# A two-block sequence model on one core: the state space branch's steps and its tiles of b and c traced in the first phase, its pairs of heads in two halves

## The chip, the cores and the metric

The kernel runs on one core of one Trainium2 chip. The metric is the device time of one execution in microseconds. Before the change the median of three runs is 3561.74 us (3559.2 to 3566.45).

## The reference

Two blocks of a hybrid sequence model follow each other on 512 tokens of width 1024. The first has three branches (state space, rwkv, hgrn), each gated and projected, then a feed-forward layer; the second has two layers of four other branches. The change touches the state space branch of the first block alone. What it computes, cut to the core:

```python
def ssd_branch(z, xbc, dt_raw, conv_w, conv_b, dt_bias, a_log, d_skip, norm_w):
    xbc = silu(centred_depthwise_conv(xbc, conv_w, conv_b))      # 5 taps, 12 tiles of 128 features
    xs, bm, cm = split(xbc, [1024, 1024 + 256])                  # x: 8 tiles, b and c: 2 tiles each
    dt = softplus(dt_raw.reshape(b, L, 2, 16) + dt_bias)         # the steps, two directions
    a = -exp(a_log)
    y_f = ssd_chunked(xs, dt[:, :, 0], a[0], bm, cm)
    y_b = flip_t(ssd_chunked(flip_t(xs), flip_t(dt[:, :, 1]), a[1], flip_t(bm), flip_t(cm)))
    y = (y_f + y_b + xs * d_skip[:, None]) * silu(z)
    return rmsnorm(y, norm_w)

def ssd_chunked(x, dt, a, bm, cm):                               # chunks of 128 tokens
    a_cum = cumsum(dt * a)
    lmat = exp(where(tril, a_cum[q] - a_cum[s], -inf))
    y_diag = (cm @ bm.T * lmat) @ (x * dt)
    chunk_states = bm.T @ (x * dt * exp(a_cum[-1] - a_cum))
    prev = scan(s -> exp(a_cum[-1]) * s + chunk_state)
    return y_diag + (cm @ prev) * exp(a_cum)
```

## The kernel before

Activations lie with features on the partitions and the 512 tokens along them, so a tile is 128 features by 512 tokens. Each matrix product splits weights and activations into a high and a low half-precision part and takes three matmuls per block of 128: a tile of projected features (`fm_g`, lines 1182 to 1193) is 24 matmuls of 128x512 over eight blocks, into one bank of PSUM. A weight unit of 512 KB holds the eight blocks; `_emit_unit` loads it on SP's queue (line 1069) and splits it into `whi` on ScalarE (line 1078) and `wlo` on VectorE (line 1079). In this phase there is one bank `acc` for foreground tiles, so the next tile starts when VectorE has read the last one. Matmuls of the background write to two banks `bg0` and `bg1`.

A scheduler lays out each engine's instructions: those traced first have priority, and later ones are put into gaps that it expects. Each engine then works through its queue in that order. Buffers of a pool go around: a new tile of a tag waits for the last reader of the buffer that it gets, and a pool that is opened over a closed one waits for its last use. Work buffers (`w`) are eight in all.

The method `first` runs the first block. The first phase is `rwkv` with `hgrn` and the gates beside it. Then its pools close and those of the branches' outputs and of the state space branch (`ssd`, line 613) open. `ssd` traces, in this order:

- The steps (lines 621 to 662): load of `wdt` on GpSimd's queue (line 1012), its split, 96 small matmuls (lines 629 to 631), the softplus in some 20 small instructions (lines 636 to 642), cumulated steps by matmuls with `tri` (line 647), totals (line 648), a transpose (line 658) and a round trip through memory: `crd` is stored (line 662) and later read back into rows (`crow`, line 690, three buffers).
- Tiles of b and c: `conv_silu` (line 602) projects a tile, scales it into a padded buffer `xp` (line 248), takes five taps (one on ScalarE, line 607, four on VectorE, line 609) and the silu (ScalarE line 610, VectorE line 611).
- The loop over eight pairs of heads: the x tile (`conv_silu`), the loads of `crow`, four transposes (line 694), four scaled copies `xd` (line 702), four masks `pm` (ScalarE lines 711 and 712, VectorE line 713), 16 products into a bank (line 720), read by line 723 into `y`; for each direction the states (lines 729 to 741), their products (line 748), scaled (lines 752 and 753) and added by GpSimd (line 754); then the z tile, read from its bank by line 757, its silu (759, 760), the product (761), the split (1239 and 1243), and the square and its sum on GpSimd (lines 764 to 768).
- The sum of squares by matmuls (line 771), its inverse root, and that as rows (lines 1320 to 1322).

Traced behind `ssd` as background is `up`: the projections of the three branches, first of rwkv's output (operands `yrh`, `yrl`), then hgrn's (`ygh`, `ygl`), 96 matmuls each, then the state space branch's own (`ysh`, `ysl`), 192 matmuls, each tile read by VectorE (lines 1354 and 1356) and added by GpSimd (line 1358). The operands of rwkv and hgrn come back from memory (`yd`, line 955), the gates too (`ug`, line 1347, two buffers). `out_ffn` follows; its first matmuls read `mh` and `ml`.

Of the kernel before, what the change touches and what calls it, by code (L numbers as in the profile page):

```python
# [78 lines left out]
def odd_even(w):  # L79
# [20 lines left out]
    + [16, 17, 18, 19] + [t + j for j in range(8) for t in (8, 0)]  # L100
# [135 lines left out]
class First:  # L236
# [365 lines left out]
    def conv_silu(self, it, n, out):  # L602

        nc, v = self.nc, self.nc.vector
        xp = self.conv_pad(self.fmx(it), 2)
# [1 line left out]
        nc.scalar.activation(out=c, in_=xp[:, 0:T], func=AF.Identity, scale=self.col("scw", n), bias=self.col("scb", n))
        for q in range(1, 5):
            v.scalar_tensor_tensor(out=c, in0=xp[:, q:q + T], scalar=self.col("scw", 12 * q + n), in1=c, op0=ALU.mult, op1=ALU.add)
        nc.scalar.activation(out=out, in_=c, func=AF.Tanh, scale=0.5)  # L610
        v.scalar_tensor_tensor(out=out, in0=out, scalar=1.0, in1=c, op0=ALU.add, op1=ALU.mult)

    def ssd(self, yh, yl):

        nc, v, mm = self.nc, self.nc.vector, self.nc.tensor.matmul
        mid, small = self.mid, self.small
        self.dsk = self.t(mid, [128, 8], "dsk")
        v.tensor_scalar(out=self.dsk, in0=self.col("sd", 0, 8), scalar1=4.0, scalar2=None, op0=ALU.mult)
        it = self.block_iter("w1", 38, 20)

        wd = self.load(mid, "wdt", [128, 8, 32], nc.gpsimd)
        wdh, wdl = self.t(mid, [128, 8, 32], "wdh", F16), self.t(mid, [128, 8, 32], "wdl", F16)
        self.split(wdh, wdl, wd, WS)
        pd = self.b("acc")
# [298 lines left out]
    def first(self, next_gain):  # L923
        parts = lambda p, n, k: (self.t(p, [128, k, T], n + "h", F16), self.t(p, [128, k, T], n + "l", F16))
        pool = self.tc.tile_pool
        if True:
            gd = self.t(self.dram, [24, 128, T], "gd", bufs=1)
            yd = self.t(self.dram, [2, 2, 128, 4, T], "yd", F16, 1)
            with self.banks(acc=1, S=2, T=1, O=1, H=1), pool(name="f_rwkv", bufs=1) as mid, pool(name="f_rwkvs", bufs=2) as small:
# [1257 lines left out]
```

## Time and profile before

| | |
|---|---|
| median of three runs | 3561.74 us (3559.2 to 3566.45) |
| the profiled execution | 3568.91 us, its span 3567.2 us, granted clock 0.974 |
| TensorE matmuls (PE) | 3344.1 us busy, 94% of the span |
| VectorE (DVE) | 2736.6 us, 77% |
| ScalarE (ACT) | 1602.6 us, 45% |
| GpSimd (POOL) | 771.2 us, 22% |
| moved by DMA | 368.16 MB, 103 GB/s |

The share of an engine is a mean over the whole span; a stretch of the branch is read from tables of that stretch. PEclk is the clock that TensorE was granted, as a part of full speed. A row of the trace gives start, length, engine, line, operation, tiles, and in brackets the engine's idle time before it with what ended it. The ends of matmuls overlap: from one start to the next is less than a matmul's own length.

### The profile page before, as it was taken

What the parts mean: (1) busy time and instruction counts of PE and PEld (TensorE: products, weight loads), DVE (VectorE), ACT (ScalarE), POOL (GpSimd) and SP (SyncE); (2) the same over time, 40 slices, a digit from 0 to 9 for tenths busy, and PEclk for the clock granted to TensorE, in tenths of its full rate; (3) what the DMA queues carried; (4) which work ended last, traced back from release to release, by engine and by line L of the source; (5) the groups of instructions that cost most, each with busy time, mean ns of one, the idle gap of its engine ahead of it and who ended that gap; (6) DMA issues with size and microseconds to landing.
All of it is one profiled execution on the core that took longest, in us unless ns stands there. A gap on an engine that the chain in (4) does not pass through costs nothing.

```text
span 3567.2 us, 60900 instructions
## 1 busy us (share of the span) xinstructions
PE 3344.1 (94%) x23806; PEld 2055.0 (58%) x23806; DVE 2736.6 (77%) x5600; ACT 1602.6 (45%) x3001; POOL 771.2 (22%) x782
## 2 busy tenths in 40 slices
PE   8999999798899998999989999999999989999998
PEld 4566666554445577656545545567656545545567
DVE  6778777578777888688877768788688867767788
ACT  4233333255444444364456534444364456534444
POOL 1222223223332212111121032221111220132211
PEclk9899999899999999999999999999999999999999
DMA  4222213133243334322323353335322323353333
GB/s 149 78 60 69 80 46 92 66 113 119 80 163 106 100 105 131 118 74 75 103 87 109 107 162 101 105 115 165 107 74 72 106 87 103 112 167 118 107 101 95
DMA packets 151156, 368.16 MB, mean 103 GB/s; under 512 B 44098, under 2 KB 47428, under 8 KB 150868
## 3 DMA queue, kind: packets, MB, share of 16 engines
q1 hardware_dynamic: 117492, 336.03, 30.4%
q0 software_dynamic: 7680, 23.00, 2.0%
q10 hardware_dynamic: 25696, 5.25, 0.8%
q8 instruction: 186, 3.05, 0.4%
q14 instruction: 102, 0.84, 0.1%
HBM read 322.72 MB, written 40.04 MB: 102 GB/s over the span
## 4 chain that ended last, share of the span: by engine, by line
PE 44%; DVE 31%; issue 8%; ACT 7%; POOL 5%; DMA 4%; ACTq 0%; SPq 0%; DVEq 0%; POOLq 0%
PE bg L1190 4%; PE bg L1191 4%; PE bg L1189 4%; PE acc L1189 3%; PE acc L1190 3%; PE acc L1191 3%; DVE wlo L1079 3%; POOL w L1464 2%; DVE bw L1118 2%; DVE w L1464 2%; PE acc L1224 1%; PE acc L1450 1%; PE acc L1449 1%; PE acc L1448 1%; PE acc L1226 1%
## 5 line engine op out<-in xcount | busy, mean ns | idle before, releaser
L1189 PE MATMUL acc<-xh,whi 128*128 128x512 f16 x1224 | 472.2, 386 | 34.5 <-DVE w L757 18.0
L1190 PE MATMUL acc<-xl,whi 128*128 128x512 f16 x1224 | 472.0, 386 | 0.0
L1191 PE MATMUL acc<-xh,wlo 128*128 128x512 f16 x1224 | 471.2, 385 | 0.0
L1078 ACT ACTIVATE whi<-wst 128x1024 f16<-128x1024 f32 x264 | 276.7, 1051 | 327.8 <-PE acc L1190 164.6
L1079 DVE SCALAR_TENSOR_TENSOR wlo<-wst,whi 128x1024 f16<-128x1024 f32 x264 | 329.6, 1249 | 32.3 <-ACT whi L1078 30.9
L1190 PEld LDWEIGHTS <-whi 128*128 128x128 f16 x1824 | 180.4, 99 | 240.2 <-issue 54.9
L1191 PEld LDWEIGHTS <-wlo 128*128 128x128 f16 x1824 | 180.3, 99 | 210.8 <-issue 15.3
L1189 PEld LDWEIGHTS <-whi 128*128 128x128 f16 x1824 | 181.3, 99 | 200.3 <-issue 11.3
L1189 PE MATMUL bg<-xh,bhi 128*128 128x512 f16 x596 | 230.1, 386 | 5.8 <-DVE hk L811 5.7
L1191 PE MATMUL bg<-xh,blo 128*128 128x512 f16 x596 | 229.8, 386 | 4.5 <-DVE reset L310 4.5
L1190 PE MATMUL bg<-xl,bhi 128*128 128x512 f16 x596 | 229.5, 385 | 0.0
L1464 POOL TENSOR_TENSOR w<-w,w 128x512 f32<-128x512 f32 x66 | 121.8, 1846 | 403.9 <-DVE w L1464 331.8
L1224 PE MATMUL acc<-whi,xh 128*128 128x128 f16 x1152 | 195.0, 219 | 4.1 <-DVE xp L1782 2.2
L1226 PE MATMUL acc<-whi,xl 128*128 128x128 f16 x1152 | 195.0, 219 | 0.0
L1225 PE MATMUL acc<-wlo,xh 128*128 128x128 f16 x1152 | 195.0, 219 | 0.0
L1078 ACT ACTIVATE bhi<-bst 128x1024 f16<-128x1024 f32 (+1 forms) x132 | 121.9, 933 | 100.5 <-PE bg L1190 86.0
L1079 DVE SCALAR_TENSOR_TENSOR blo<-bst,bhi 128x1024 f16<-128x1024 f32 (+1 forms) x132 | 155.5, 1182 | 6.8 <-ACT bhi L1078 5.8
L1189 PE MATMUL bg<-xh,whi 128*128 128x512 f16 x408 | 158.1, 387 | 0.5 <-ACT bw L1334 0.5
L1190 PE MATMUL bg<-xl,whi 128*128 128x512 f16 x408 | 157.9, 387 | 0.0
L1191 PE MATMUL bg<-xh,wlo 128*128 128x512 f16 x408 | 157.7, 386 | 0.0
L1190 PEld LDWEIGHTS <-bhi 128*128 128x128 f16 x980 | 97.2, 99 | 105.0 <-issue 15.5
L1191 PEld LDWEIGHTS <-blo 128*128 128x128 f16 x980 | 96.8, 99 | 103.1 <-issue 7.1
(685 smaller groups left out, 9227.5 us busy)
## 6 DMA issues: line engine op xcount, KB each, us to landing
wst<-win SPq DMA_DIRECT2D x92, 512.0 KB, 3.5
bst<-win SPq DMA_DIRECT2D x64, 512.0 KB, 3.7
wst<-wff SPq DMA_DIRECT2D x60, 512.0 KB, 3.5
wst<-w SPq DMA_DIRECT2D x58, 512.0 KB, 3.6
gd<-bw SPq DMA_DIRECT2D x88, 256.0 KB, 2.1
ug<-gd SPq DMA_DIRECT2D x88, 256.0 KB, 2.8
wst<-wf SPq DMA_DIRECT2D x30, 512.0 KB, 3.4
bst<-w SPq DMA_DIRECT2D x20, 512.0 KB, 4.1
```

Source lines behind the costliest of these rows:

```text
L1078: nc.scalar.activation(out=hi[:, h], in_=st[:, h], func=AF.Copy, scale=WS)
L1079: nc.vector.scalar_tensor_tensor(out=lo[:, h], in0=st[:, h], scalar=WS, in1=hi[:, h], op0=ALU.mult, op1=ALU.subtract)
L1118: nc.vector.tensor_tensor(out=src, in0=x, in1=y, op=ALU.add if m == 1 else ALU.subtract)
L1189: mm(ps, lhsT=wh, rhs=h[:, k, :], start=(k == 0), stop=False)
L1190: mm(ps, lhsT=wh, rhs=l[:, k, :], start=False, stop=False)
L1191: mm(ps, lhsT=wl, rhs=h[:, k, :], start=False, stop=(k == nk - 1))
L1224: mm(o, lhsT=xh, rhs=wh, start=(k == 0), stop=False)
L1225: mm(o, lhsT=xh, rhs=wl, start=False, stop=False)
L1226: mm(o, lhsT=xl, rhs=wh, start=False, stop=(k == 7))
L1448: mm(ps, lhsT=ah[:, p], rhs=bh, start=start and p == 0, stop=False)
L1449: mm(ps, lhsT=ah[:, p], rhs=bl, start=False, stop=False)
L1464: tt = lambda eng, o, x, y, op=ALU.add: eng.tensor_tensor(out=o, in0=x, in1=y, op=op)
```

## The change

`conv_silu` is taken apart: `scaled` reads the tile from its bank into a work buffer, `conv` takes the five taps with shortened ranges at the ends and no pad, `silu2` does the silu. `ssd_begin` is called while the first phase's pools are open: it traces the steps, with work buffers and a bank of the first phase, loads `wdt` and `tri` on SP, and traces the tiles of b and c up to their taps. `ssd` takes these over, loads its own `tri`, and traces each pair's entry (x tile, rows, transposes, scaled copies) ahead of the pair before it; `xd` has eight buffers. The units of `w1` are reordered for this. The read-out of z gets high priority, and the squares move from GpSimd to ScalarE.

```diff
-    + [16, 17, 18, 19] + [t + j for j in range(8) for t in (8, 0)]
+    + [16, 17, 18, 19, 8] + [t + j for j in range(7) for t in (9, 0)] + [7]
...
-    def conv_silu(self, it, n, out):
-        xp = self.conv_pad(self.fmx(it), 2)
...
+    def scaled(self, it):
+        x = self.w()
+        self.nc.vector.tensor_tensor(out=x, in0=self.fmx(it), in1=self.rb, op=ALU.mult)
+        return x
+    def conv(self, x, n):
+        nc, v = self.nc, self.nc.vector
         c = self.w()
...
+        nc.scalar.activation(out=c, in_=x, func=AF.Identity, scale=self.col("scw", 24 + n), bias=self.col("scb", n))
+        for q in (0, 1, 3, 4):
+            to, by = slice(max(2 - q, 0), T - max(q - 2, 0)), slice(max(q - 2, 0), T - max(2 - q, 0))
+            v.scalar_tensor_tensor(out=c[:, to], in0=x[:, by], scalar=self.col("scw", 12 * q + n), in1=c[:, to], op0=ALU.mult, op1=ALU.add)
+        return c
...
-    def ssd(self, yh, yl):
+    def ssd_begin(self):
...
-        wd = self.load(mid, "wdt", [128, 8, 32], nc.gpsimd)
+        wd = self.w(256).rearrange("p (k c) -> p k c", k=8)
+        nc.sync.dma_start(out=wd, in_=self.io["wdt"])
...
-        pd = self.b("acc")
+        pd = self.b("S")
...
-        tri = self.load(mid, "tri", [128, 2, 128])
+        tri = self.w(256).rearrange("p (d c) -> p d c", d=2)
+        nc.sync.dma_start(out=tri, in_=self.io["tri"])
...
+        return it, (dt, cum, dec, tot, crd), [self.conv(self.scaled(it), 8 + n) for n in range(4)]
+    def ssd(self, yh, yl, begun):
+        it, (dt, cum, dec, tot, crd), bcx = begun
...
+        tri = self.load(mid, "tri", [128, 2, 128])
...
-            self.conv_silu(it, 8 + n, bc[:, n])
+            self.silu2(bcx[n], bc[:, n])
...
-        for j in range(8):
+        def enter(j):
             g = j // 4
             x = self.t(mid, [128, T], "xs", bufs=2)
-            self.conv_silu(it, j, x)
+            self.silu2(self.conv(self.scaled(it), j), x)
...
-                    t = self.t(mid, [128, T], "xd", bufs=4)
+                    t = self.t(mid, [128, T], "xd", bufs=8)
...
+            return x, crow, xd, xe
+        nxt = enter(0)
+        for j in range(8):
+            g = j // 4
+            x, crow, xd, xe = nxt
+            if j < 7:
+                nxt = enter(j + 1)
...
-            v.tensor_tensor(out=z, in0=pz, in1=self.rb, op=ALU.mult)
+            with self.tc.high_priority():
+                v.tensor_tensor(out=z, in0=pz, in1=self.rb, op=ALU.mult)
...
-                nc.gpsimd.tensor_tensor(out=sq, in0=y, in1=y, op=ALU.mult)
+                nc.scalar.activation(out=sq, in_=y, func=AF.Square)
...
                 beside(1000, 1000)
+                begun = self.ssd_begin()
...
-                    rbs = self.ssd(*ysm)
+                    rbs = self.ssd(*ysm, begun)
```

Where instructions stand is shown at three places. Lines of the kernel after lie some 30 further down: its 1101 is 1069 before, 987 is 955, 1221 is 1189, and in the loop 724 is 702, 753 is 723, 771 is 741, 783 is 753, 788 is 757.

TensorE's queue at the end of the first phase, before. `H` is the hgrn's bank, `T` that of the rwkv's last transposes, `xh` the operand of the steps' matmuls:

```order
L887 MATMUL H_6707<-hi_5719,hw_6705 128x128 x3
L584 MATMUL T_6603<-ident_75,M_5957 128x128 x4
L904 MATMUL H_6715<-hi_5719,hs_6170 128x128
L908 MATMUL H_6715<-hst_6711,hp_5578 128x128
```

The same place in the kernel after; `acc_6919` is the bank of b's first tile:

```order
L918 MATMUL H_6707<-hi_5719,hw_6705 128x128 x3
L1221 LDWEIGHTS whi_6534
L1221 MATMUL acc_6919<-xh,whi_6534 128x512
L1222 LDWEIGHTS whi_6534
L1222 MATMUL acc_6919<-xl,whi_6534 128x512
L584 MATMUL T_6603<-ident_75,M_5957 128x128
L1223 LDWEIGHTS wlo_6535
L1223 MATMUL acc_6919<-xh,wlo_6535 128x512
```

All 24 matmuls of b's first tile stand now between the rwkv's last chunk and the hgrn's last products (line 904 before, 935 after); the other three tiles of b and c stand behind the steps, and behind 32 matmuls of `up` that precede line 647.

SP's queue at the same time, before; `yd` holds the outputs of rwkv and hgrn in memory:

```order
L598 DMA yd_184<-w_6612 128x512
L599 DMA yd_184<-w_6613 128x512
L1012 DMA tri_6914<-tri 128x256
L955 DMA yrh_6760<-yd_184 128x2048
L598 DMA yd_184<-gyh_6740 128x512
L599 DMA yd_184<-gyl_6741 128x512
L955 DMA yrl_6761<-yd_184 128x2048
```

After:

```order
L598 DMA yd_184<-w_6612 128x512
L599 DMA yd_184<-w_6613 128x512
L631 DMA w_6751<-wdt 128x256
L1044 DMA tri_7098<-tri 128x256
L987 DMA yrh_7083<-yd_184 128x2048
L598 DMA yd_184<-gyh_6740 128x512
L599 DMA yd_184<-gyl_6741 128x512
L987 DMA yrl_7084<-yd_184 128x2048
```

The load of `wdt` has come to SP's queue, ahead of the first load into the new pools; the loads of `yrh` and `yrl` stand where they stood.

VectorE's queue in the loop, around the fourth pair's scaled copies, before (`xd`, `sst` and `sec` are all of the same pair):

```order
L611 SCALAR_TENSOR_TENSOR xs_7727<-xs_7727,w_7763 128x512
L702 TENSOR_TENSOR xd_7780<-T_7775,dt_6878 128x512
L702 TENSOR_TENSOR xd_7782<-T_7775,dec_6881 128x512
L702 TENSOR_TENSOR xd_7784<-T_7775,dt_6878 128x512
L702 TENSOR_TENSOR xd_7786<-T_7775,dec_6881 128x512
L736 COPY sst_7839<-S_7835 128x128
L741 SCALAR_TENSOR_TENSOR sst_7839<-sst_7839,tot_6927,S_7835 128x64 x4
L753 TENSOR_TENSOR sec_7852<-sec_7852,O_7845 128x384
```

After, around the fifth pair's copies; `sy_7878` and `sec_7897` are the fourth pair's, `w_7955` is its z tile:

```order
L621 SCALAR_TENSOR_TENSOR xs_7774<-xs_7774,w_7808 128x512
L753 SCALAR_TENSOR_TENSOR sy_7878<-xs_7582,dsk_7096,O_7861 128x512
L724 TENSOR_TENSOR xd_7825<-T_7820,dt_6854 128x512
L724 TENSOR_TENSOR xd_7827<-T_7820,dec_6856 128x512
L724 TENSOR_TENSOR xd_7829<-T_7820,dt_6854 128x512
L788 TENSOR_TENSOR w_7955<-acc_7924,rb_166 128x512
L724 TENSOR_TENSOR xd_7831<-T_7820,dec_6856 128x512
L783 TENSOR_TENSOR sec_7897<-sec_7897,O_7890 128x384
```

The copies of the next pair stand among the work of this one, and the read-out of z stands among the copies. Between the read-out of the first x tile and the sum of squares TensorE's queue held 220 matmuls of `up`; now it holds 106, with 58 before it (18 then) and 220 behind (146 then).

## Rows read from the trace of the kernel before

**Rows 1.** Busy time of each engine in four stretches; its first row names the columns
```profile
core 0: us, PE busy (x) PEld busy (x) DVE busy (x) ACT busy (x) POOL busy (x), PEclk, DMA share, GB/s
676.00:704.70 28.70, 13.54 (x138) 10.67 (x139) 10.04 (x42) 4.10 (x14) 7.62 (x11) 0.52 0.39 127
704.70:740.60 35.90, 35.00 (x178) 17.72 (x177) 30.83 (x59) 17.38 (x34) 3.19 (x13) 1.00 0.42 143
740.60:975.60 235.00, 206.06 (x1162) 114.74 (x1160) 182.37 (x289) 116.61 (x240) 73.05 (x67) 0.94 0.31 99
975.60:1013.30 37.70, 36.20 (x162) 17.31 (x163) 24.00 (x31) 10.88 (x15) 17.07 (x11) 0.91 0.37 119
```

**Rows 2.** TensorE in order of time at the hand-over; start, length, in brackets idle before
```profile
682.24 1.72 PE L584 MATMUL T<-ident,M 128*128 128x128 f32 x4 [3.08 <-DVE M L578]
...
693.84 1.09 PE L1571 MATMUL H<-ident,hw 128*128 128x128 f32 x4 [4.08 <-DVE hw L918]
...
700.63 0.21 PE L629 MATMUL acc<-wdh,xh 128*128 128x32 f16 x1 [5.71 <-ACT wdh L1239]
```

**Rows 3.** SP's queue in order of time, then DMA issues with KB and time to landing
```profile
688.92 0.32 SPq L599 DMA_DIRECT2D yd<-w  x1
...
696.92 0.42 SPq L955 DMA_DIRECT2D yrl<-yd  x1
...
yrl<-yd SPq DMA_DIRECT2D x1, 512.0 KB, 5.1
...
wdt<-wdt POOLq DMA_DIRECT2D x1, 128.0 KB, 4.9
```

**Rows 4.** TensorE in order of time: one tile's first and last matmul, what follows
```profile
704.74 0.38 PE L1189 MATMUL acc<-xh,whi 128*128 128x512 f16 x1
...
709.70 0.38 PE L1191 MATMUL acc<-xh,wlo 128*128 128x512 f16 x1
...
711.55 0.38 PE L1189 MATMUL acc<-xh,whi 128*128 128x512 f16 x1 [0.61 <-DVE xp L248]
...
713.35 1.96 PE L647 MATMUL O<-da,tri 128*128 128x16 f32 x16
```

**Rows 5.** First x tile read out, first matmul for the sum of squares, first of `out_ffn`
```profile
740.58 0.69 DVE L248 TENSOR_TENSOR xp<-acc,rb 128x512 f32<-128x512 f32 x1
...
975.57 1.05 PE L771 MATMUL T<-ones,sqa 128*128 128x1 f32 x8 [1.66 <-POOL sqa L768]
...
1013.35 0.38 PE L1189 MATMUL acc<-mh,whi 128*128 128x512 f16 x1
```

**Rows 6.** TensorE's groups from 740.6 to 975.6: busy us, mean ns, idle before, releaser
```profile
L1189 PE MATMUL acc<-xh,whi 128*128 128x512 f16 x120 | 48.8, 407 | 18.2 <-DVE w L757 18.0
...
L694 PE MATMUL T<-ident,xs 128*128 128x128 f32 x32 | 6.0, 320 | 7.3 <-DVE xs L611 7.2
```

**Rows 7.** VectorE's groups from 700 to 977, and line 761's first and last start
```profile
L753 DVE TENSOR_TENSOR sec<-sec,O 128x384 f32<-128x384 f32 x16 | 8.9, 554 | 11.4 <-PE O L748 7.9 <-ACT sec L752 3.5
...
L1079 DVE SCALAR_TENSOR_TENSOR blo<-bst,bhi 128x512 f16<-128x512 f32 x8 | 6.3, 782 | 0.0
L723 DVE SCALAR_TENSOR_TENSOR sy<-xs,dsk,O 128x512 f32<-128x512 f32 x8 | 6.0, 748 | 15.1 <-PE O L720 15.1
L761 DVE SCALAR_TENSOR_TENSOR sy<-sy,w 128x512 f32<-128x512 f32 x8 | 5.5, 687 | 4.9 <-POOL sy L754 4.9
...
L1356 DVE SCALAR_TENSOR_TENSOR mg<-ug,bg 128x512 f32<-128x512 f32 x8 | 5.4, 678 | 0.0
...
L761 DVE SCALAR_TENSOR_TENSOR sy<-sy,w x8: 677/692/693, 772.3 to 972.0; 128x512 f32<-128x512 f32 x8
```

**Rows 8.** GpSimd's squares as a group; one of them and a VectorE operation beside it
```profile
L767 POOL TENSOR_TENSOR w<-sy 128x512 f32<-128x512 f32 x7 | 10.6, 1514 | 6.5 <-DVE sy L761 6.5
...
797.76 1.95 POOL L767 TENSOR_TENSOR w<-sy 128x512 f32<-128x512 f32 x1 [1.24 <-DVE sy L761]
...
798.74 1.52 DVE L713 TENSOR_TENSOR pm<-pm,cb 128x512 f32<-128x512 f32 x1
```

More of the change, by code (lines that the diff above doesn't have):

```diff
@@ L599, in store @@
         self.nc.sync.dma_start(out=yd[1, :, j], in_=l)
-    def conv_silu(self, it, n, out):
+    def scaled(self, it):
[3 more added lines that the diff above has]
+    def conv(self, x, n):
         nc, v = self.nc, self.nc.vector
-        xp = self.conv_pad(self.fmx(it), 2)
         c = self.w()
[L607 to L611, printed above, removed]
@@ L613, in ssd, with silu2 @@
-    def ssd(self, yh, yl):
+        nc.scalar.activation(out=c, in_=x, func=AF.Identity, scale=self.col("scw", 24 + n), bias=self.col("scb", n))
[3 more added lines that the diff above has]
+        return c
+    def silu2(self, c, out):
+        self.nc.scalar.activation(out=out, in_=c, func=AF.Tanh, scale=0.5)
+        self.nc.vector.scalar_tensor_tensor(out=out, in0=out, scalar=1.0, in1=c, op0=ALU.add, op1=ALU.mult)
@@ L615, in ssd @@
+    def ssd_begin(self):
         nc, v, mm = self.nc, self.nc.vector, self.nc.tensor.matmul
-        mid, small = self.mid, self.small
-        self.dsk = self.t(mid, [128, 8], "dsk")
-        v.tensor_scalar(out=self.dsk, in0=self.col("sd", 0, 8), scalar1=4.0, scalar2=None, op0=ALU.mult)
         it = self.block_iter("w1", 38, 20)
-        wd = self.load(mid, "wdt", [128, 8, 32], nc.gpsimd)
-        wdh, wdl = self.t(mid, [128, 8, 32], "wdh", F16), self.t(mid, [128, 8, 32], "wdl", F16)
-        self.split(wdh, wdl, wd, WS)
@@ L624, in ssd @@
-        pd = self.b("acc")
+        flat = lambda a: a.rearrange("p k c -> p (k c)")
+        wd = self.w(256).rearrange("p (k c) -> p k c", k=8)
+        nc.sync.dma_start(out=wd, in_=self.io["wdt"])
+        wdh, wdl = (self.w(256, dt=F16).rearrange("p (k c) -> p k c", k=8) for _ in range(2))
+        self.split(flat(wdh), flat(wdl), flat(wd), WS)
+        pd = self.b("S")
         for i in range(4):
@@ L631, in ssd @@
                 mm(o, lhsT=xl, rhs=wdh[:, k], start=False, stop=(k == 7))
-        sm = lambda tag: self.t(small, [128, 4, 32], tag, bufs=1)
-        dt, da, cum, dec = sm("dt"), sm("da"), sm("cum"), sm("dec")
+        sm = lambda tag: self.t(self.norms, [128, 4, 32], tag)
+        dt, cum, dec, tot = sm("dt"), sm("cum"), sm("dec"), sm("tot")
+        da = self.w(128).rearrange("p (i c) -> p i c", i=4)
         fl = lambda a: a.rearrange("p i c -> p (i c)")
@@ L649, in ssd @@
         v.tensor_copy(out=fl(cum), in_=pc[:, 0:128])
-        tot = self.t(small, [128, 4, 32], "tot", bufs=1)
         v.tensor_copy(out=fl(tot), in_=pc[:, 128:256])
@@ L655, in ssd @@
         nc.scalar.activation(out=fl(tot), in_=fl(tot), func=AF.Exp)
-        pr = self.b("T")
+        pr = self.b("S")
         for i in range(4):
@@ L662, in ssd @@
         nc.gpsimd.dma_start(out=crd, in_=cr[0:32])
+        return it, (dt, cum, dec, tot, crd), [self.conv(self.scaled(it), 8 + n) for n in range(4)]
+    def ssd(self, yh, yl, begun):
+        nc, v, mm = self.nc, self.nc.vector, self.nc.tensor.matmul
+        mid, small = self.mid, self.small
+        it, (dt, cum, dec, tot, crd), bcx = begun
+        self.dsk = self.t(mid, [128, 8], "dsk")
+        v.tensor_scalar(out=self.dsk, in0=self.col("sd", 0, 8), scalar1=4.0, scalar2=None, op0=ALU.mult)
+        tri = self.load(mid, "tri", [128, 2, 128])
         bc = self.pwide(mid, "bc", 4)
@@ L763, in ssd @@
             if j == 0:
-                nc.gpsimd.tensor_tensor(out=sqa, in0=y, in1=y, op=ALU.mult)
+                nc.scalar.activation(out=sqa, in_=y, func=AF.Square)
             else:
                 sq = self.w()
-                nc.gpsimd.tensor_tensor(out=sq, in0=y, in1=y, op=ALU.mult)
+                nc.scalar.activation(out=sq, in_=y, func=AF.Square)
                 nc.gpsimd.tensor_tensor(out=sqa, in0=sqa, in1=sq, op=ALU.add)
@@ L1684, in values, with log_sigmoid @@
         return v
-    def log_sigmoid(self, out, f, n):
+    def log_sigmoid(self, out, f, n, t=None):
         nc, v = self.nc, self.nc.vector
-        t = lambda tag: self.t(self.small, [128, n], tag, bufs=1)
+        t = t or (lambda tag: self.t(self.small, [128, n], tag, bufs=1))
         a, s, w, p = t("lsa"), t("lss"), t("lsw"), t("lsp")
```

4 lines of the change are left out of this document (2 added, 2 removed).

## The prediction, made before the kernel after had run

> **What bounds the kernel now.** I first read the busy table by stretch [rows 1], cut at four events of the branch: the hand-over from the first phase (676 to 704.7 us), the steps and the tiles of b and c (to 740.6, where the branch's first x tile is read out of its bank), the loop over eight pairs (to 975.6, the matmuls of the sum of squares), and the tail of `up` (to 1013.3, where `out_ffn` begins). The built instructions stand in the same order on every engine before and after this region in both kernels, so the prediction is a sum over these stretches. TensorE is the engine that all wait for. It is busy 13.5 of 28.7 us in the hand-over, 35.0 of 35.9 in the second stretch, 206.1 of 235.0 in the loop, 36.2 of 37.7 in the tail. What can be won is its idle time, 28.9 us of the loop and about 15 of the hand-over, and what it does at the lower clock there (granted 0.52 in the hand-over, 0.94 in the loop). Second I read who ends the idle time. In the hand-over TensorE waits for the end of the rwkv and hgrn chains and last for `wdt`, 5.71 us [rows 2], because that load is issued behind the release of the first phase's pools and takes 4.9 us [rows 3]. In the loop the idle time before the tile matmuls is 18.2 us, 18.0 of it until line 757 has read the z tile out of the single acc bank; 7.3 us more come before the transposes of x [rows 6]. Third, VectorE: 182.4 us of 235 in the loop [rows 1], and it waits too, 15.1 us for the heads' matmuls, 11.4 for the states' (line 753), 4.9 for GpSimd (line 761) [rows 7]. One pair follows another every (972.0 - 772.3) / 7 = 28.5 us [rows 7], and no engine fills it: a pair's chain is too serial.
>
> **The hand-over.** A tile is 24 matmuls, and from the first to the last of a tile 23 starts take 4.96 us [rows 4], so 0.216 us each and 5.2 us a tile. The order now puts b's first tile between the transposes of line 584 and the hgrn matmuls, where TensorE idles 3.08 and 4.08 us at 0.5 clock and more [rows 2]. I cost it at nothing there; in twice the time, if the clock stays low, it would still fit, with at most some 1 us of delay for the chain. `wdt` is now loaded by SP right behind the yd store of 688.92 [rows 3] and lands, by the old 4.9 us, before 694. The 96 matmuls of the steps then wait only for the hgrn transpose (693.84) and the split on ScalarE behind it; by the transpose's 1.09 [rows 2] and, as an estimate, 1.3 for the two reads and the split behind it, they start at 696.2 and not 700.63: 4.4 us earlier. That is not all won: the next on TensorE's queue are matmuls of `up`, and their operand yrl is still issued at 696.92 and lands 5.1 us later [rows 3], at 702.0; its pool still waits for the first phase. So TensorE idles once more, some 2.7 us. Then 32 of these matmuls (6.9 us) precede line 647: 708.9, not 713.35 [rows 4], again 4.4 us earlier, bounded by TensorE's queue and not by VectorE. What is late next is the read-out of b's first tile. Its w buffer is the one that da held, so it comes behind the steps, about 713.9, and b's second tile starts at 714.0 where before it started at 711.55 [rows 4]. From that start to the read-out of the first x tile took 740.58 - 711.55 = 29.0 us [rows 4, 5], of which some 3 were line 647's and 658's own matmuls, now done: 26.0. **x's first tile is read out at 740.0, 0.6 us earlier.** But 58 matmuls of `up` are done by then, and 18 before.
>
> **The loop.** On TensorE the order leaves 106 matmuls of `up` in it, where 220 stood: 114 fewer, -24.6 us. Work: 206.1 - 24.6 = 181.5 us. The waits: the z read-out has high priority now, and TensorE has the next pair's x tile around it. Bounds: all 28.9 us stay, or none does. I replace the 18.0 by the least that such a read-out cost, 0.61 us [rows 4], eight times (4.9), and keep the other 10.9: 15.8. Loop by TensorE: 197.3 us. On VectorE: six read-outs of `up` fewer at 0.68 (line 1356) and six halves of weights fewer at 0.78 (line 1079) [rows 7] are -4.1 and -4.7. The squares leave GpSimd for ScalarE, which has room (116.6 us of 235 [rows 1]). When a square ran on GpSimd from 797.76 for 1.95 us, line 713 took 1.52 us from 798.74 [rows 8]; an operation of this size takes 0.69 (line 761 [rows 7]). The 0.83 for each of eight squares are -6.6; bounds 0 and the squares' whole time, 8 x 1.514 = 12.1 us [rows 8]. 182.4 - 4.1 - 4.7 - 6.6 = 167.0. Of its 52.6 us of waiting I keep those on a producer that still stands right ahead, 15.1 and 4.9, and 4.7 that no row names, and drop those for states, transposes and x tiles, since they now belong to the next pair and stand several rows ahead: 191.7. TensorE's 197.3 is the longer and holds; a pair then takes 24 us, not 28.5. Eight xd buffers let the next pair's copies be made before this pair's have been read. The conv's pad is gone with its memsets; its taps are the same five instructions. The second load of tri, and a weight remainder of `up` that now stands before crd on GpSimd's queue, I cost at nothing: tri is wanted at 708.9, crd at 713. **Loop: -37.7 us**; the sum of squares comes at 937.3, not 975.57 [rows 5].
>
> **The tail.** What left the loop has to be done here: 220 matmuls of `up` follow (220 x 0.216 = 47.5 us), 146 before. Before, it took 1013.35 - 975.57 = 37.8 us [rows 5], 31.5 of it for 146 matmuls; of the other 6.3, 1.5 were waits (36.2 busy of 37.7) and (1 - 0.91) x 37.7 = 3.4 the lower clock [rows 1]. Both go, since matmuls over yg now cover the chain from the sum of squares to its rows; 1.4 stays. 47.5 + 1.4 = 48.9: **+11.1 us.** `out_ffn` starts at 986.2.
>
> **Sum:** -0.6 - 37.7 + 11.1 = -27.2 us. The profiled execution took 3568.9 (span 3567.2, 1.7 outside it); it would take 3541.7. The median of the three runs is 7.2 lower, 3561.7, which gives 3534.5: **3535 us**.
>
> **A rule beside it.** The Trainium skill, "SBUF — State Buffer" (section "SBUF: two separate sides"), says that VectorE, in an operation with two SBUF inputs, and GpSimd share a port pair that one of them holds for its whole instruction, while the other waits. The trace agrees in kind: 1.52 us against 0.69 [rows 7, 8]. By the rule, as an estimate, a square could cost VectorE its full length, and the sum would be that of the second rival.
>
> **The rivals.** *The loop keeps its waits.* If TensorE's 28.9 us of idle time only change place, since there is still one acc bank and one for transposes, the loop is 181.5 + 28.9 = 210.4 us: -0.6 - 24.6 + 11.1 = -14.1, 3548 us. For it: each engine works in its queue's order, and two pairs in it only help where the order guessed durations right. *The squares held VectorE for their whole length.* Then 12.1 us go, VectorE's sum falls to 186.2, and with it those waits of TensorE that VectorE ends: 181.5 + 4.9 = 186.4 us, -0.6 - 48.6 + 11.1 = -38.1 in all, 3524 us. Against it: line 713 lost 0.83 of 1.95. *Slower: the filler is spent early.* `up` filled the loop, and 40 of its matmuls are now gone before x. If a pair's time is set by its own chain (heads, GpSimd's additions, then z) at 28.5 us whatever the order, the loop stays at 235 and the tail has grown: -0.6 + 11.1 = +10.5, 3572 us. It decides from a loop of 224.5 us, 27.2 a pair. For it: GpSimd's additions and the fourth pm still wait in turn, and crow has three buffers as before. Against it: VectorE's own 167 us leave a pair at 21. That the change doesn't do what it says is no rival of its own: the order shows it done.
>
> **How the numbers follow.** My forecast (3528 to 3543) has 0.50, the loop that keeps its waits (3543 to 3556) 0.22, the whole squares 0.15, and what lies above, no change or slower, 0.13. Two in ten left out: 3521 to 3557. About 0.2%, 7.1 us, is what a measurement of this kernel tells from no change: a loop under 217 us is faster (0.85), one of 217 to 231 is the same (0.08), a longer one slower (0.07).
>
> **What would show it.** In the profile after: `wdt` landing before 694 and the steps' matmuls at 696; a wait of some 2.7 us for yrl in front of `up`; line 647's matmuls near 709; the wait for the z read-out down from 18 us to about 5; a pair every 24 us; the sum of squares near 937 and `out_ffn` near 986; line 713 close to 0.7 us on average. I am wrong if the pairs still take 27 us or more, if TensorE waits in the loop for weights or for crow, or if the tail waits for weights of wbs rather than running through.

## The result and the profile after

| | before | after |
|---|---|---|
| median of seven runs each, us | 3566.45 (3559.2 to 3577.13) | 3532.95 (3517.86 to 3544.5) |
| ratio, with its 95% interval | | 0.9898, 0.988 to 0.9917 |
| profiled execution, us | 3568.91 | 3532.95 |
| its span, us | 3567.2 | 3531.2 |
| predicted, us | | 3535 (3521 to 3557) |

The kernel after is 1.0% faster, and its time is within 2 us of the forecast. The forecast change was smaller, -26.7 us from the 3561.74 known then; by the seven runs of each it is -33.5. That it came so near is partly luck: three terms of the sum were wrong by 4 to 14 us and largely cancelled.

Busy time of each engine in the kernel after, cut at the events of [rows 1]: the hand-over, the steps and the tiles of b and c up to the first x tile's read-out, the loop, the tail up to `out_ffn`.

```profile
core 0: us, PE busy (x) PEld busy (x) DVE busy (x) ACT busy (x) POOL busy (x), PEclk, DMA share, GB/s
676.00:704.70 28.70, 17.94 (x160) 11.28 (x158) 15.11 (x55) 5.31 (x16) 7.63 (x6) 0.71 0.49 156
704.70:744.30 39.60, 36.68 (x185) 18.36 (x183) 31.88 (x51) 19.49 (x37) 4.91 (x6) 0.99 0.48 158
744.30:927.80 183.50, 175.47 (x1050) 100.61 (x1048) 156.12 (x276) 112.43 (x238) 47.23 (x42) 0.99 0.30 98
927.80:981.80 54.00, 51.17 (x237) 24.23 (x237) 32.96 (x39) 15.19 (x20) 25.06 (x16) 0.97 0.45 146
```

The events themselves in order of time, answering to [rows 5], and below them the durations and the first and last start of line 792 (761 before), answering to the last of [rows 7]:

```profile
744.32 0.69 DVE L605 TENSOR_TENSOR w<-acc,rb 128x512 f32<-128x512 f32 x1
...
927.80 1.05 PE L802 MATMUL T<-ones,sqa 128*128 128x1 f32 x8
...
981.83 0.38 PE L1221 MATMUL acc<-mh,whi 128*128 128x512 f16 x1
```

```profile
L792 DVE SCALAR_TENSOR_TENSOR sy<-sy,w x8: 679/692/694, 775.4 to 924.4; 128x512 f32<-128x512 f32 x8
```

The first x tile is read out 3.7 us later than before, the loop takes 183.5 us and not 235.0, the tail 54.0 and not 37.8: -31.5 us up to `out_ffn`. A pair takes (924.4 - 775.4) / 7 = 21.3 us, 28.5 before. The other 4.5 us by which the spans differ lie behind `out_ffn`, in code that did not change; that part took 2553.8 us before, 2549.4 here and 2555.9 in a second profile of the kernel after, so it is no effect of the change.

In the loop, TensorE's and VectorE's groups that answer to [rows 6] and [rows 7] (busy us, mean ns, idle before, releaser):

```profile
L1221 PE MATMUL acc<-xh,whi 128*128 128x512 f16 x120 | 45.6, 380 | 1.1 <-DVE w L605 1.1
...
L750 PE MATMUL O<-pm,xd 128*64 128x128 f32 x256 | 31.2, 278 | 1.5 <-DVE pm L743 0.7 <-ACT ysh L1271 0.4 <-ACT w L798 0.3
L778 PE MATMUL O<-bc,sst 128*64 128x128 f32 x192 | 23.7, 283 | 1.8 <-DVE sst L771 1.8
...
L1223 PE MATMUL bg<-ygh,blo 128*128 128x512 f16 x22 | 8.9, 415 | 2.8 <-DVE blo L1111 2.8
...
L743 DVE TENSOR_TENSOR pm<-pm,cb 128x512 f32<-128x512 f32 x30 | 21.0, 713 | 1.1 <-ACT pm L742 1.1
...
L615 DVE SCALAR_TENSOR_TENSOR w<-w,cols,w 128x510 f32<-128x510 f32 x16 | 13.9, 866 | 0.9 <-ACT w L612 0.8
L615 DVE SCALAR_TENSOR_TENSOR w<-w,cols,w 128x511 f32<-128x511 f32 x16 | 11.9, 742 | 0.0
...
L1275 DVE SCALAR_TENSOR_TENSOR ysl<-sy,cols,ysh 128x512 f16<-128x512 f32 x8 | 7.8, 978 | 0.0
...
L753 DVE SCALAR_TENSOR_TENSOR sy<-xs,dsk,O 128x512 f32<-128x512 f32 x8 | 6.0, 748 | 15.9 <-PE O L750 15.9
```

The 18.2 us in front of the tile matmuls are 1.1 and no longer end with z. The same 120 matmuls are shown with a mean of 380 ns, 407 before, and the granted clock of the loop is 0.99, not 0.94. One pause of TensorE in the loop of the kernel before, and what follows it:

```profile
916.77 0.38 PE L1189 MATMUL bg<-ygh,bhi 128*128 128x512 f16 x1
919.55 0.59 PE L1189 MATMUL acc<-xh,whi 128*128 128x512 f16 x1 [2.40 <-DVE w L757]
919.93 0.63 PE L1190 MATMUL acc<-xl,whi 128*128 128x512 f16 x1
920.36 0.63 PE L1191 MATMUL acc<-xh,wlo 128*128 128x512 f16 x1
...
922.78 0.38 PE L1191 MATMUL acc<-xh,wlo 128*128 128x512 f16 x1
922.99 0.38 PE L1189 MATMUL acc<-xh,whi 128*128 128x512 f16 x1
```

Behind the pause the matmuls start 0.43 us apart, at the lower of the clock's two levels (1.2 GHz), and at the end 0.21 us apart again (2.4 GHz). With 8.0 us of pauses in the loop and not 28.9, less of it runs at the lower level. VectorE still waits 15.9 us for the heads' matmuls (line 753, 723 before).

### The profile page after: what moved, and what is told of

Same layout as the page of the kernel before. It is cut to its first block, busy times and chain, and to the rows that moved or that the text cites. A ratio compares the mean times of both kernels' runs of the same rounds, so it can differ in the third digit from the quotient of the medians.

```text
span 3531.2 us, 60877 instructions
## 1 busy us (share of the span) xinstructions
PE 3334.8 (94%) x23806; PEld 2048.1 (58%) x23806; DVE 2727.1 (77%) x5600; ACT 1606.4 (45%) x3009; POOL 753.5 (21%) x749
## 4 chain that ended last, share of the span: by engine, by line
PE 28%; DVE 23%; ACT 5%; issue 5%; POOL 4%; DMA 2%; DVEq 0%; POOLq 0%; ACTq 0%; SPq 0%
PE bg L1223 3%; PE bg L1222 3%; PE bg L1221 3%; DVE wlo L1111 2%; PE acc L1221 2%; PE acc L1222 2%; PE acc L1223 2%; DVE bw L1150 2%; POOL w L1496 2%; DVE w L1496 1%; PE acc L1256 1%; PE acc L1257 1%; PE acc L1258 1%; PE S L1637 1%; DVE blo L1111 1%
## 5 line engine op out<-in xcount | busy, mean ns | idle before, releaser
L1496 POOL TENSOR_TENSOR w<-w,w 128x512 f32<-128x512 f32 x66 | 121.8, 1846 | 403.2 <-DVE w L1496 331.4
L1111 DVE SCALAR_TENSOR_TENSOR blo<-bst,bhi 128x1024 f16<-128x1024 f32 (+1 forms) x132 | 160.6, 1221 | 7.4 <-ACT bhi L1110 6.3
```

The costliest lines, as they stand in the source:

```text
L1111: nc.vector.scalar_tensor_tensor(out=lo[:, h], in0=st[:, h], scalar=WS, in1=hi[:, h], op0=ALU.mult, op1=ALU.subtract)
L1496: tt = lambda eng, o, x, y, op=ALU.add: eng.tensor_tensor(out=o, in0=x, in1=y, op=op)
```

## The experiments

All cut the trace at the same four events: the first transpose of line 584, the read-out of the first x tile, the sum of squares, the first matmul of `out_ffn`. The last column but two counts the matmuls of `up` that stand behind the sum of squares in the built order. Ratios are to the kernel before, run on the same chip.

| kernel | start to x, us | loop | tail | whole stretch | `up` behind | median, us | ratio (95%) |
|---|---|---|---|---|---|---|---|
| before | 58.3 | 235.0 | 37.8 | 331.1 | 146 | 3566.45 | |
| after | 62.1 | 183.5 | 54.0 | 299.6 | 220 | 3532.95 | 0.9898 (0.988 to 0.9917) |
| after_again | 61.9 | 184.0 | 52.6 | 298.5 | 220 | 3535.82 | 0.9921 (0.9906 to 0.9936) |
| one_pair | 62.1 | 220.0 | 37.9 | 320.1 | 141 | 3558.54 | 0.9982 (0.9963 to 1.0002) |
| sq_on_gpsimd | 61.4 | 190.1 | 54.4 | 305.8 | 223 | 3537.33 | 0.9931 (0.9908 to 0.9954) |
| begin_late | 59.7 | 181.7 | 64.5 | 305.8 | 265 | 3541.49 | 0.9934 (0.9911 to 0.9957) |
| z_in_turn | 62.8 | 181.8 | 50.9 | 295.6 | 215 | 3525.79 | 0.9885 (0.9848 to 0.9923) |
| xd_four | 61.9 | 183.3 | 52.6 | 297.8 | 220 | 3532.70 | 0.991 (0.9883 to 0.9936) |
| extra_squares | 61.2 | 191.7 | 52.6 | 305.4 | 220 | 3544.20 | 0.994 (0.9916 to 0.9963) |
| before_sq_scalar | 58.9 | 231.0 | 38.1 | 328.0 | 143 | 3562.76 | 0.9992 (0.9979 to 1.0006) |
| before_z_first | 57.8 | 235.3 | 38.4 | 331.4 | 146 | 3570.32 | 1.0013 (0.9994 to 1.0032) |
| add_vector_z_turn | 64.2 | 181.0 | 52.3 | 297.4 | 215 | 3530.69 | 0.99 (0.9873 to 0.9927) |
| first_z_turn | 60.5 | 184.4 | 52.9 | 297.7 | 215 | 3526.52 | 0.9896 (0.9879 to 0.9914) |
| all_first_z_turn | 67.8 | 186.9 | 40.9 | 295.7 | 177 | 3526.83 | 0.9898 (0.9882 to 0.9913) |

> The kernel after, unchanged, beside the next three on one chip. Expected by every theory: the stretch from the transposes of line 584 to out_ffn within 2 us of the first trace's 299.6, the loop within 1 us of 183.5, ratio 0.988 to 0.992.

The stretch is a sharper measure than the time: runs of one kernel are 6 to 36 us apart, and the unchanged code behind the stretch alone took 2547.6 to 2556.6 us in these traces. Three traces have the order of the kernel after (xd_four is one, below): 299.6, 298.5 and 297.8, mean 298.6, so a difference under 2 us says nothing.

**The halves undone.** The order of the units of `w1` goes back with them.

```diff
...
-            x, crow, xd, xe = nxt
-            if j < 7:
-                nxt = enter(j + 1)
+            x, crow, xd, xe = enter(j)
```

> The kernel after with one edit undone: each pair's x tile, rows, transposes and scaled copies are traced at its own turn (and the units of w1 ordered for it), the rest as after. Theory 1 (the two halves of a pair took the waits out of the loop): a pair takes 27 to 28.5 us again instead of 21.3, the loop 215 to 235 instead of 183.5; up leaves the filler in the loop again, so the tail is shorter by some 15; time 3550 to 3565 us. Theory 2 (the squares on ScalarE and the early read-out of z took them out): the pair stays near 22, time within 5 us of the kernel after (3533).

Its loop in the table by stretch, then TensorE's groups in it:

```profile
741.80:961.82 220.02, 194.88 (x1130) 110.23 (x1128) 171.66 (x283) 117.76 (x244) 54.37 (x46) 0.97 0.30 97
```

```profile
L1218 PE MATMUL acc<-xh,whi 128*128 128x512 f16 x120 | 47.3, 395 | 10.6 <-DVE w L605 5.5 <-DVE w L785 5.0
...
L716 PE MATMUL T<-ident,xs 128*128 128x128 f32 x32 | 5.1, 281 | 4.7 <-DVE xs L621 4.7
L1218 PE MATMUL bg<-ysh,bhi 128*128 128x512 f16 x8 | 3.4, 430 | 6.7 <-ACT ysh L1268 6.5 <-DVE ug L1385 0.2
```

The waits are back: 25.1 us of idle time, 8.0 in the kernel after, before x tiles, z tiles, transposes and `up`. A pair takes 27.2 us. The whole stretch is 21.5 us longer than the mean of after: two thirds of the gain are the halves. Theory 1 holds, with early steps, squares and z still in place.

**The squares back on GpSimd.**

```diff
-                nc.scalar.activation(out=sq, in_=y, func=AF.Square)
+                nc.gpsimd.tensor_tensor(out=sq, in0=y, in1=y, op=ALU.mult)
```

> The kernel after with the squares of y back on GpSimd, nothing else. Theory 1 (the loop is now TensorE's, 175 of 183.5 us busy, and VectorE has 27 us to spare): VectorE's sum in the loop rises by 6 to 12 us, the loop by at most 4, time 3533 to 3538 us. Theory 2 (the squares held VectorE for their whole length and this was the larger part of the gain): the loop rises by the eight squares, 12 us or more, time 3545 to 3552.

VectorE's sum in the loop rose from 156.1 to 164.1 us, inside theory 1's 6 to 12, but the loop by 6.6, more than the 4 that it allowed: VectorE's 27 us of idle time did not swallow the 8. Theory 2's 12 us or more did not come. The stretch lost 7.2 us; the median, 3537.3, lies in theory 1's range.

**One more square on GpSimd, which nobody reads.**

```diff
+            sx = self.t(mid, [128, T], "sx", bufs=2)
+            nc.gpsimd.tensor_tensor(out=sx, in0=y, in1=y, op=ALU.mult)
```

> The kernel after with one more square of y for each pair on GpSimd into a buffer that nobody reads; the squares that count stay on ScalarE. The disputed cost by itself: what a GpSimd operation costs that no instruction waits for. Theory 1 (as forecast from line 713, a square costs VectorE about half its own length): VectorE's sum in the loop is 156.1 + 8 x 0.83 = 163 us, the loop within 4 us of 183.5. Theory 2 (it holds VectorE for its whole length): 156.1 + 8 x 1.5 = 168 us. Theory 3 (it costs VectorE nothing, and the squares cost only through the additions that wait behind them on GpSimd's queue): 156 to 158 us.

TensorE's and ScalarE's built orders are those of the kernel after; VectorE's and SP's differ only by an instruction at the hand-over. So this is what the operation alone does to the loop. The loop's table, then groups of VectorE and GpSimd in it:

```profile
748.51:940.16 191.65, 176.36 (x1051) 100.54 (x1049) 164.10 (x276) 112.95 (x239) 58.53 (x50) 0.99 0.29 95
```

```profile
L743 DVE TENSOR_TENSOR pm<-pm,cb 128x512 f32<-128x512 f32 x30 | 25.7, 869 | 1.1 <-ACT pm L742 1.1
...
L1277 DVE SCALAR_TENSOR_TENSOR ysl<-sy,cols,ysh 128x512 f16<-128x512 f32 x8 | 11.5, 1431 | 0.0
...
L792 DVE SCALAR_TENSOR_TENSOR sy<-sy,w 128x512 f32<-128x512 f32 x8 | 5.5, 688 | 4.4 <-POOL sy L784 4.4
L788 DVE TENSOR_TENSOR w<-acc,rb 128x512 f32<-128x512 f32 x8 | 5.5, 685 | 0.3 <-PE acc L1225 0.2
...
L795 POOL TENSOR_TENSOR sx<-sy 128x512 f32<-128x512 f32 x8 | 10.9, 1366 | 4.1 <-DVE sy L792 4.0
```

One pair's VectorE, and GpSimd at the same time (line 801 adds up the squares):

```profile
823.35 2.13 DVE L743 TENSOR_TENSOR pm<-pm,cb 128x512 f32<-128x512 f32 x2
825.40 1.82 DVE L1277 SCALAR_TENSOR_TENSOR ysl<-sy,cols,ysh 128x512 f16<-128x512 f32 x1
```

```profile
823.71 1.23 POOL L795 TENSOR_TENSOR sx<-sy 128x512 f32<-128x512 f32 x1
825.40 1.27 POOL L801 TENSOR_TENSOR sqa<-sqa,w 128x512 f32<-128x512 f32 x1 [0.47 <-ACT w L800]
```

Eight squares of 10.9 us together cost VectorE 164.1 - 156.1 = 8.0 us, 0.73 of their own length: between theory 1 (163) and theory 2 (168), nearer to 1. Theory 3's 156 to 158 did not come, and VectorE's wait for GpSimd's additions (line 792) is 4.4 us as in the kernel after. Nearly all of it is in two lines whose operands are all in SBUF: line 743 went from 713 to 869 ns (4.7 us in sum), line 1275, here 1277, from 978 to 1431 ns (3.7). They have not the same cause. Line 743 ran beside the squares, and of the two operations above the second took 1.52 us and not 0.68, as in [rows 8]. Line 1277 ran beside the addition of line 801, which in the kernel after mostly started behind it: the extra square moved the two onto each other. So 0.73 is the net price in this loop; beside the square itself VectorE lost the forecast's 0.83 us or so. Line 788, which reads a bank, ran beside GpSimd's arithmetic in four of its eight times and took 686 ns then, 683 otherwise. The loop took all of it, +8.2 us, and not the 4 that theory 1 allowed, although no instruction reads the squares; TensorE's idle time in it grew from 8.0 to 15.3 us. The Trainium skill, "SBUF — State Buffer" (section "SBUF: two separate sides"), has a VectorE operation with two SBUF inputs and a GpSimd operation exclude each other for a whole instruction on the ports that they share; lines 743, 1277 and 788 agree with that.

**Squares alone, in the kernel before.** The same edit as the change's, nothing else.

> The kernel before with the squares moved to ScalarE alone. Theory 1 (there a pair is a chain through all engines, of which the square is no step, so only what VectorE loses beside it comes off): VectorE's sum in the loop falls by 6 to 12 us, the pair of 28.5 to 27.5 or more, the stretch up to out_ffn by 2 to 8 us (the kernel after with the squares put back lost 6.2), ratio 0.998 to 0.9995. Theory 2 (the squares bound the loop of the kernel before): that stretch falls by 12 us or more, ratio under 0.997.

VectorE's sum in the loop fell by 6.3 us (182.4 to 176.1), the pair to 28.15 us, the stretch by 3.1. Theory 1. GpSimd's sum fell by 11.9 (73.1 to 61.1), so here a us of its work cost VectorE 0.53 and not 0.73.

**Early steps undone.** `ssd_begin` is called in front of `ssd`, in the second phase's pools.

```diff
                 beside(1000, 1000)
-                begun = self.ssd_begin()
...
+                    begun = self.ssd_begin()
                     rbs = self.ssd(*ysm, begun)
```

> The kernel after with the steps and the tiles of b and c traced behind the first phase's pools, where they stood before; halves, squares and z as after. Theory 1 (as forecast, the early steps let 40 more matmuls of up go before x, which is worth their 8.6 us less the 3.7 us by which x came later): time 3536 to 3541. Theory 2 (filler that is spent early is missing in the loop, so the early steps win nothing): the loop holds more of up and has no more waits, out_ffn begins within 2 us of the kernel after, time 3531 to 3535.

Its three tables by stretch (start to x, loop, tail):

```profile
671.68:731.33 59.65, 50.92 (x322) 28.42 (x323) 40.65 (x81) 22.84 (x49) 8.43 (x9) 0.84 0.46 149
731.33:913.04 181.71, 166.93 (x1026) 97.84 (x1023) 154.25 (x275) 112.37 (x238) 42.44 (x37) 0.98 0.29 97
913.04:977.52 64.48, 60.58 (x281) 28.70 (x282) 34.36 (x43) 16.44 (x23) 30.67 (x20) 0.97 0.45 145
```

Here x comes 2.4 us sooner, and the stretch is yet 7.2 us longer. The loop is the telling row: TensorE does 8.5 us less in it than in the kernel after, and it is only 1.8 us shorter. So TensorE's load does not set the loop; a pair takes 20.8 us with 8.5 us less of TensorE's work beside it. What does not fit beside the pairs goes behind: 45 more matmuls of `up`, 45 x 0.216 = 9.7 us, and the tail is 10.5 us longer. Theory 1's sign, and its time 0.5 us past the end of its range; its explanation held for the filler, but the part of it in the loop counted more than the part before x. Theory 2 falls.

**z in its turn, and z first in the kernel before.**

```diff
-            with self.tc.high_priority():
-                v.tensor_tensor(out=z, in0=pz, in1=self.rb, op=ALU.mult)
+            v.tensor_tensor(out=z, in0=pz, in1=self.rb, op=ALU.mult)
```

> The kernel after with the read-out of z at the priority of its place, nothing else. Theory 1 (as forecast, the priority is what shortened the wait before the tile matmuls): that wait, 1.1 us in the loop of the kernel after, comes back to 10 us or more, time 3541 to 3548. Theory 2 (with the next pair's x tile traced ahead of it the read-out is early anyhow): the wait stays under 5 us, time within 4 us of 3533.

> The kernel before with the read-out of z at high priority, nothing else. Theory 1 (as forecast: the read-out's place on VectorE's queue makes TensorE's 18.0 us of waiting for the acc bank): the wait falls to about 5 us and the stretch up to out_ffn by 5 to 13 us, ratio 0.996 to 0.999. Theory 2 (VectorE reaches z late because the pair's own chain is late, whatever the place): the wait turns into others, the stretch stays within 3 us of 331, ratio 0.999 to 1.001.

Without the priority the wait before the tile matmuls is 0.1 us; the stretch is 3.0 us shorter than after's mean. Theory 2 by the wait, and the priority if anything costs; the median, 3525.8, is 7 us under 3533, where theory 2 allowed 4, but the ratios' intervals overlap, so no gain in time is shown. In the kernel before, the priority won nothing, ratio 1.0013 (0.9994 to 1.0032). TensorE's groups in its loop, to be held against [rows 6]:

```profile
L1190 PE MATMUL acc<-xh,whi 128*128 128x512 f16 x120 | 47.1, 393 | 18.7 <-DVE xp L248 11.7 <-DVE w L758 6.9
...
L694 PE MATMUL T<-ident,xs 128*128 128x128 f32 x32 | 6.3, 332 | 10.3 <-DVE xs L611 10.3
```

The wait for z fell from 18.0 to 6.9 us, and the x tile's read-out, which nothing had waited for, took over 11.7; the one before the transposes grew from 7.3 to 10.3. Theory 2, its ratio just past its end: the 18 us were the pair's chain showing up at the single bank, and z's place in the queue only chose where.

**Four xd buffers.** `"xd", bufs=8` becomes `bufs=4`.

> The kernel after with four xd buffers instead of eight. Theory 1 (as forecast: the overlap lives from making the next pair's copies before this pair's are read): the copies of line 724 wait for the states' matmuls, a pair goes back to 25 us or more, time 3550 to 3560. Theory 2 (the copies stand late enough in VectorE's order that four are free by then): the wait in front of line 724 stays under 5 us in the loop, the pair under 22.5, time within 6 us of the kernel after (3533).

The built order of this stretch is the same on every engine, line 724 waits 0.8 us in both, the loop is 183.3 us. Theory 2: the four further buffers do nothing.

**Tries at a faster kernel.** In add_vector_z_turn line 784's additions move to VectorE; in first_z_turn b's first tile is read out ahead of the steps, in all_first_z_turn all four tiles of b and c with their taps; all three read z in its turn.

```diff
+        bcx = [self.conv(self.scaled(it), 8 + n) for n in range(4)]
         flat = lambda a: a.rearrange("p k c -> p (k c)")
...
-        return it, (dt, cum, dec, tot, crd), [self.conv(self.scaled(it), 8 + n) for n in range(4)]
+        return it, (dt, cum, dec, tot, crd), bcx
```

> A try at a faster kernel: the kernel after with z read out in its turn (4 us faster up to out_ffn than with priority, by the traces) and the additions of line 784 on VectorE instead of GpSimd. Theory 1 (what GpSimd runs costs VectorE more than it saves, and the chain of a pair loses two crossings): VectorE's sum in the loop stays within 5 us of 155 although it has 16 additions of 0.55 more, the loop falls under 181, time 3522 to 3529 us. Theory 2 (VectorE becomes the engine that TensorE waits for): VectorE's sum reaches 163 or more, the loop 186 or more, time over 3532.

> A try at a faster kernel, and a test of the step on b's first tile: z in its turn, and the read-out of b's first tile traced ahead of the steps, so that its buffer and its place on VectorE's queue are no longer behind them and b's second tile stands in TensorE's pause before the hgrn transposes. Theory 1 (the buffer and the order held the read-out back, as forecast; TensorE's 4.5 us of idle time there are to be had): the read-out comes near 690 instead of 716, x's first tile 3 to 6 us earlier, the stretch up to out_ffn 291 to 294 us, time 3522 to 3528. Theory 2 (what is won there is lost behind it, since the steps and the chain of softplus still bound the loop's first rows): 295 to 298 us, time 3528 to 3534.

> As the one before, with all four tiles of b and c, read-outs and taps, traced ahead of the steps. Theory 1 (the steps have slack, since the first rows of crow are wanted late): the stretch up to out_ffn 290 to 294 us. Theory 2 (the steps and crow are then late for the first pair, and up has to fill: 103 of its matmuls stand ahead of the first transposes of x in TensorE's order, 64 in the one before): 298 us or more, time over 3532.

With the additions on VectorE its sum is 156.4 us although it has 16 operations of 0.55 more (154.5 in z_in_turn), while GpSimd's fell from 50.0 to 29.1; the loop is 181.0, where theory 1 begins, but that is only 0.8 less than z_in_turn's, and the time, 3530.7, lies between the theories. No gain is shown. In first_z_turn the read-out comes at 693.77, and TensorE's pause before the hgrn transposes is gone:

```profile
694.51 0.38 PE L1221 MATMUL acc<-xh,whi 128*128 128x512 f16 x1 [1.93 <-DVE w L605]
697.22 0.63 PE L1603 MATMUL H<-ident,hw 128*128 128x128 f32 x4 [0.18 <-DVE hw L949]
```

Yet x comes only 1.4 us sooner than in after_again, and the stretch is 0.8 shorter: theory 2 by the trace, while the median, 9.3 us under after_again's on the same chip, lies in theory 1's range. Where the median's difference sits is open; the profiled run was the slowest of the six. The kernel that differs from it by the early read-out alone is z_in_turn: beside that one x comes 2.3 us sooner, and the stretch is 2.1 longer. all_first_z_turn lies between its theories, with 295.7 us: x comes 5.9 us later than in after_again, but 43 more matmuls of `up` are done before the tail, which is 40.9 us. Beside after_again its five runs took 3522.4 to 3530.1 us, the six of after_again 3531.5 to 3537.8. Of the two tried beside the kernel after it is the one whose every run beats every run of that; by the medians that is 0.25%. How much of it is z in its turn is not shown: z_in_turn's stretch is 295.6 us as well, and it ran on another chip.

## Why the prediction was right, point by point

**The hand-over: right up to line 647, wrong behind it.** `wdt` was issued at 691.25 and landed 2.4 us later, before 694 as forecast; the steps' matmuls began at 695.75 (forecast 696.2); the operand yrl came at 701.55 (702.0). The wait for it was 1.14 us and not 2.7, since two matmuls on `yrh` stood ahead of it. TensorE in order of time, the issue of `wdt` on SP's queue, and its size and time to landing:

```profile
695.75 0.18 PE L639 MATMUL S<-w,xh 128*128 128x32 f16 x1 [1.08 <-ACT w L1271]
...
699.40 1.01 PE L1221 MATMUL bg<-yrh,bhi 128*128 128x512 f16 x2
701.55 0.59 PE L1222 MATMUL bg<-yrl,bhi 128*128 128x512 f16 x1 [1.14 <-DMA yrl<-yd]
...
704.06 0.63 PE L1222 MATMUL bg<-yrl,bhi 128*128 128x512 f16 x1
704.49 0.63 PE L1223 MATMUL bg<-yrh,blo 128*128 128x512 f16 x1
...
711.48 1.96 PE L659 MATMUL O<-w,w 128*128 128x16 f32 x16 [1.54 <-DVE w L653]
```

```profile
691.25 0.44 SPq L631 DMA_DIRECT2D w<-wdt  x1
```

```profile
w<-wdt SPq DMA_DIRECT2D x1, 128.0 KB, 2.4
```

Then "bounded by TensorE's queue and not by VectorE" failed. Line 659 (647 before) stood at 711.48, not 708.9, and waited 1.54 us for VectorE, whose softplus ended with line 653; until 704.9 the matmuls of `up` also started only every 0.43 us (704.06, 704.49), at the lower level of the clock, and not every 0.216. From there to x it took 1.7 us more than forecast. x: 744.3, not 740.0, an error of +4.3. That b's first read-out, late behind the steps, was what held x is also refuted: counted from line 584 first_z_turn read it 27 us sooner, and x 1.4.

**The loop: right in direction, -51.5 and not -37.7.** The work of TensorE was 175.5 us, not 181.5: I took 24.6 off a sum made at a clock of 0.94 and left the clock there. The waits were 8.0, not 15.8: the 10.9 that I kept beside z's, without a reason, shrank as well. VectorE's sum was 156.1, not 167.0. The six read-outs that left with `up` are 4.0 of its fall of 26.3, as forecast; the six halves are 3.0 and not 4.7, since the two that stayed take 1641 ns each, not 782. The other 19.3, where I had 6.6, is operations that became shorter. The squares are 6.3 to 8.0 of it, by before_sq_scalar and extra_squares (bounds 0 and 12.1). The rest I had no term for: the taps, 34.7 us before, are 25.8 in the two rows of line 615. Their shortest and median lengths did not change, only the longest; durations (shortest, median, longest, in ns) of line 609 before, then of line 615 after:

```profile
L609 DVE SCALAR_TENSOR_TENSOR w<-xp,cols,w x32: 735/747/3142, 743.0 to 951.3; 128x512 f32<-128x512 f32 x32
```

```profile
L615 DVE SCALAR_TENSOR_TENSOR w<-w,cols,w x32: 735/744/1754, 746.9 to 893.8; 128x510 f32<-128x510 f32 x16, 128x511 f32<-128x511 f32 x16
```

Nine of the 32 taps took over 1 us before, three after, and each of these has arithmetic of GpSimd beside it in time: weight halves and additions of `up`, the sum of squares, an addition of line 754; none has a square. GpSimd's sum in the loop went from 73.1 to 47.2 us, and its eight squares were only 12.1 of these 25.8; three additions (4.8) and two weight halves of `up` (5.3) left the loop with its matmuls. So GpSimd's part of `up` left with it, a term that the prediction put at nothing. How much VectorE loses for a us of GpSimd is no constant: 0.73 in extra_squares, 0.53 in before_sq_scalar, 0.33 in add_vector_z_turn beside z_in_turn (154.5 + 8.8 - 156.4 = 6.9 for 20.9). What GpSimd's part of `up` cost VectorE in all was not tried by itself.

**"TensorE's 197.3 is the longer and holds" was the wrong model.** The loop is neither engine's sum. It took on VectorE's 8.0 us whole while VectorE was idle for 27 (extra_squares), and it hardly changed when TensorE had 8.5 us less to do (begin_late). What fits both is the chain of a pair through TensorE and VectorE, overlapped with the next pair's first half: 21 us a pair, and `up` fills what it leaves. The steps of that chain were not timed one by one.

**z and xd: reasons that were not needed.** I gave the z read-out's priority a part in cutting 18.0 to 4.9; the tracing order does it alone, to 0.1. The eight xd buffers are idle.

**The tail: +16.2, not +11.1.** 47.5 us for 220 matmuls was right. The rest, 1.4, was mis-sized: the matmuls for the sum of squares and its rows take 1.05 and 2.1 us by themselves, and their two waits stayed:

```profile
932.34 0.46 PE L1353 MATMUL T<-w,ones 128*128 128x128 f32 x2 [1.30 <-DVE w L1352]
934.33 1.65 PE L1353 MATMUL T<-w,ones 128*128 128x128 f32 x6 [1.53 <-DVE w L1352]
```

**The sum.** +4.3, -13.8 and +5.1 leave -4.4 of error: -31.5 measured against -27.2. By undoing each part from the mean of after's traces: halves 21.5 us, squares 7.2, early steps 7.2, z's priority -3.0, xd nothing; 32.9, where 331.1 - 298.6 = 32.5 is to be explained. The parts add up, but not because each has a price of its own: put into the kernel before, the squares won 3.1 us and z's priority nothing. The taps without a pad were not undone.

**The rivals.** *The loop keeps its waits* is refuted (8.0 us and not 28.9). *The squares held VectorE for their whole length* gave the nearest loop, 186.4, for a reason that carries 7 to 8 of 51.5 us. *Filler spent early* had the right thought, a loop set by the pair's own chain, and the wrong length for it: with the halves overlapping 21.3 us, not 28.5, far under its break-even of 27.2.

## What to carry to other kernels

An idle engine in front of a bank is often the end of a chain, not a late read-out: giving the read-out priority moved 11.7 us of waiting to the next read-out, and only tracing the next pair's first half ahead took it away. When a loop is a chain, filler beside it is nearly free until it no longer fits (8.5 us for 1.8), and then it costs its full time behind the loop; count what is left for the tail. Sum the work at the clock that the loop will have, not at the one that its pauses gave it.

## What had not been expected of the hardware

A GpSimd operation whose result no instruction reads cost VectorE 0.73 of its length and the loop 8.2 us for 10.9 us of such work, with VectorE idle for 27 us of it. Only two lines grew clearly, both with all operands in SBUF (713 to 869 and 978 to 1431 ns), one beside the extra work, the other beside a GpSimd addition that had been moved onto it. An operation that reads a bank did not grow beside GpSimd's (686 and 683 ns, line 788).
